# Latent attention's scores as one product over 128 rows a head

## The chip, the cores and the metric

The kernel runs on one core of a Trainium2 chip. Its time is device microseconds (us) from launch to end, the median of several runs; a profiled execution gives the rows below. Engines are named as in the profile: PE is TensorE's matmul stream and PEld its weight loads, DVE is VectorE, ACT is ScalarE, POOL is GpSimd, SP is SyncE, whose queue issues nearly all loads.

## The reference, cut to what matters

The model has two parts. The first is two layers on 256 tokens of width 1024. Each layer projects x by `w_in` (kept in HBM as streamed weights) and mixes three groups: a gated recurrence of 8 heads (HGRN2), latent attention of 8 heads (MLA), and cross-attention of 4 heads into a memory. Then comes an output product and a layer norm. The second part is one block of dilated attention and pooling, followed by a retrieval layer that gathers expert rows (8 heads of 16 for each token). Only the latent attention of the two layers is changed:

```python
q = (_rmsnorm(cq, q_norm) @ w_uq).reshape(B, S, 8, 64 + 32)
q_nope, q_rope = q[..., :64], _rope(q[..., 64:], cos, sin)
c = _rmsnorm(ckv, kv_norm)
k_nope = (c @ w_uk).reshape(B, S, 8, 64)
v = (c @ w_uv).reshape(B, S, 8, 64)
k_rope = _rope(kr, cos, sin)                  # one rotary key for all heads
s = (einsum('bqhd,bkhd->bhqk', q_nope, k_nope)
     + einsum('bqhr,bkr->bhqk', q_rope, k_rope)) / sqrt(96)
# causal mask, softmax, product with v
```

`_rope` multiplies the two halves of the 32 rotary channels by cosine and sine: `[t1*cos - t2*sin, t1*sin + t2*cos]`.

## The kernel before, in words

All weights of `w_in`, `w_out` and the memory projections come from HBM in half units of 128x1024 fp32 (512 KB), by SP, into `raw` (three buffers). ACT rounds each to `wh` (line 158), DVE forms the rest `wl` (line 159), and PE makes three products per pair of tiles from them (lines 212 to 214, `mm3`). `feature` (line 224) gives feature-major results, `token` (line 240) token-major ones. This stream of weights sets the order of the program.

Everything else in a layer is side work: Python generators in a list, `self.side`, that hand out instructions in pieces and name a cost for each piece (`yield 0.6`). Each half unit calls `tick`, which adds a credit of 1.4 (`PACE_A`) and takes pieces from the head of the list until the credit is spent. `finish(task)` writes out at once all that is left up to a task. `behind` (`bh` in the code) orders a DVE instruction behind the latest `wl` split on that engine. The final order on each engine is made by a list scheduler that goes by program order and modelled readiness.

For a layer the list starts with `mla_qkv` and `mla_rest` (projections of the latent attention), then the first recurrence pair, then `mla_attend`, later `finish(o0)` writes out what is left of `mla_attend`, of the second recurrence pair and of its output.

`mla_rest` transposes the normed latent rows into `cT` (line 498) and makes, from weights `ws` loaded once per layer: queries without rotation `qn` and rotary queries `qr`, six banks' halves of 128 columns (line 511, evicted by ACT at 513 and 515); keys `kn` (line 521) and values `v` (line 526), evicted by ACT; then it swaps the rotary halves of `qr` with a permutation product (line 531) and rotates on DVE (lines 535 to 538); then it transposes the rotary key (line 542), repeats it over 128 rows straight and swapped (lines 546, 547) and rotates it into `kr` (lines 550 to 552). PSUM banks come from `pps`, which has two.

`mla_attend` goes through `attend` eight times a layer: for each of the two query tiles of 128 tokens (`tt`), four groups of two heads, with 128 keys for the first tile and 256 for the second. A group's scores are two products a head, into one bank: 64 rows of `qn` and `kn` (line 562), then 32 rows of `qr` and `kr` (line 564) on top. DVE adds the causal mask (line 569), reduces and so on; transposes (436) and the product with `v` (460) follow.

An fp32 product stands as two PE records in the trace. `lnr`, the norm's rows for the end of the layer, shares the buffer of `ws` and is loaded by SP once the last product with `ws` is done (line 640).

Of the kernel before, what the change touches and what calls it, by code (L numbers as in the profile page):

```python
# [8 lines left out]
F = mybir.dt.float32  # L9
# [3 lines left out]
AF = mybir.ActivationFunctionType  # L13
OP = mybir.AluOpType
# [4 lines left out]
S = 256  # L19
D = 1024  # L20
# [76 lines left out]
def pack(inp):  # L97

    g = {k: np.asarray(v) for k, v in inp.items()}
    o = {}  # L100
    o["ca"], o["cb"] = _shape_constants()
    o["x"] = g["x"].reshape(2, 128, D).transpose(1, 0, 2)
    o["memT"] = g["mem"][0].T.reshape(8, 128, S).transpose(1, 0, 2)
    o["pos"] = g["positions"].reshape(1, S)
    wu, wm, ws = [], [], []
    for l in range(NL):
        w = g["w_in"][l]
        m = w[:, OCQ:OMG].reshape(2, 4, 128, 416).transpose(0, 2, 1, 3).reshape(2, 128, 1664)
        wm.append(m)
        u = _fm(g["w_mem_k"][l], 0, 512) + _tm(g["w_mem_v"][l], 0, 512)  # L110
        pair = lambda j: _fm(w, OF + 256 * j, 256) + _fm(w, OQ + 256 * j, 256)
        u += pair(0) + _tm(w, OI, 512) + pair(1) + _tm(w, OG, 512) + pair(2) + _tm(w, OI + 512, 512) + pair(3)
        u += _fm(w, OMQ, 512) + _tm(w, OG + 512, 512) + _tm(w, OMEMG, 512) + _tm(w, OMG, 512)
        wo = g["w_out"][l].reshape(4, 4, 128, 2, 512)
        for kg in KORD:
            for cg in range(2):
                u.append(wo[kg, :, :, cg].transpose(1, 0, 2).reshape(128, 2048))
        wu.append(np.stack(u))
        uq = g["w_mla_uq"][l].reshape(2, 128, 8, 96)
        uq = np.concatenate([uq[..., :64].reshape(2, 128, 512), uq[..., 64:].reshape(2, 128, 256)], axis=-1)  # L120
        ws.append(np.concatenate([uq.transpose(1, 0, 2).reshape(128, 1536), g["w_mla_uk"][l], g["w_mla_uv"][l]], axis=1))
    o["wu"], o["wm"], o["ws"] = np.stack(wu), np.stack(wm), np.stack(ws)
    o["rows1"] = np.concatenate([g["hgrn_out_norm"], g["mla_q_norm"], g["mla_kv_norm"], g["ln_g"], g["ln_b"]], axis=1)
    o["lnc"] = np.stack([g["ln_g"], g["ln_b"]], axis=1).reshape(2, 2, 8, 128).transpose(3, 0, 1, 2)
    o["lbl"] = g["hgrn_lb_logits"].reshape(2, 8, 128).transpose(2, 0, 1)
    cols = [g["c_2"].reshape(8, 128).T, g["norm1_g_2"].reshape(8, 128).T, g["norm2_g_2"].reshape(8, 128).T,
            g["pool_scale_2"].reshape(4, 128).T, g["b_ada_2"].reshape(48, 128).T]
    o["cols2"] = np.concatenate(cols, axis=1)
    o["rows2"] = np.concatenate([g["b_ada_2"][0, 2048:3072], g["b_ada_2"][0, 5120:6144], g["final_g_2"]]).reshape(1, 3072)
    o["wada"] = g["w_ada_2"][0].reshape(8, 128, 6, 1024).transpose(2, 0, 1, 3)  # L130
    w2 = g["w_in_2"][0]
    u = _fm(w2, 0, 1024) + _tm(w2, 1024, 1024)
    wo = g["w_out_2"][0].reshape(2, 4, 128, 2, 512)
    for kg in (1, 0):
        for cg in range(2):
            u.append(wo[kg, :, :, cg].transpose(1, 0, 2).reshape(128, 2048))
    u += _fm(g["peer_wq_2"][0], 0, 2048)
    o["wu2"] = np.stack(u)
    o["ws2"] = np.concatenate([g["pool_w_2"][0].transpose(1, 0, 2).reshape(128, 512),
                               g["peer_subkeys_2"][0].transpose(2, 0, 1).reshape(128, 256)], axis=1)  # L140
    o["puv"] = np.concatenate([g["peer_u_2"][0], g["peer_v_2"][0]], axis=1)
    return {k: np.ascontiguousarray(v) for k, v in o.items()}


class Prog:
# [346 lines left out]
    def mla_rest(self, ws, cn, out):  # L492
        nc, bh = self.nc, self.behind
        cT = self.ml.tile([128, 3, S], F, name="cT")
        for k in range(3):
            ps = self.pps.tile([128, S], F, name="bank")
# [1 line left out]
                nc.tensor.transpose(ps[:, tt * 128:(tt + 1) * 128], cn[:, tt, k * 128:(k + 1) * 128], self.ident)  # L498
            nc.scalar.activation(cT[:, k, :], ps, AF.Copy)
            yield 0.3  # L500
        sc = 1.0 / math.sqrt(96)
        qn = self.ml.tile([128, 4, S], F, name="qn")
        qr = self.ml.tile([128, 2, S], F, name="qr")
        kn = self.ml.tile([128, 4, S], F, name="kn")
        v = self.ml.tile([128, 2, 512], F, name="v")
        for j in range(3):
            ps = self.pps.tile([128, 2, S], F, name="bank")
            for m in range(2):
                for k in range(2):
                    c = k * 768 + (2 * j + m) * 128  # L510
                    nc.tensor.matmul(ps[:, m, :], ws[:, c:c + 128], cT[:, k, :], start=k == 0, stop=k == 1)
            if j < 2:
                nc.scalar.activation(qn[:, 2 * j:2 * j + 2, :], ps, AF.Copy, scale=sc)
            else:
                nc.scalar.activation(qr, ps, AF.Copy, scale=sc)
            yield 0.6
        for j in range(2):
            ps = self.pps.tile([128, 2, S], F, name="bank")
            for m in range(2):
                c = 1536 + (2 * j + m) * 128  # L520
                nc.tensor.matmul(ps[:, m, :], ws[:, c:c + 128], cT[:, 2, :], start=True, stop=True)
            nc.scalar.activation(kn[:, 2 * j:2 * j + 2, :], ps, AF.Copy)
            yield 0.6
        for tt in range(2):
            ps = self.pps.tile([128, 512], F, name="bank")
            nc.tensor.matmul(ps, cT[:, 2, tt * 128:(tt + 1) * 128], ws[:, 2048:2560], start=True, stop=True)
            nc.scalar.activation(v[:, tt, :], ps, AF.Copy)
            yield 0.6

        ps = self.pps.tile([128, 2, S], F, name="bank")  # L530
        nc.tensor.matmul(ps, self.perm, qr, start=True, stop=True)
        tmp = self.h2.tile([128, 2, S], F, name="pt")
        sb = self.sin[:, None, :].to_broadcast([128, 2, S])
        cb = self.cos[:, None, :].to_broadcast([128, 2, S])
        bh(nc.vector.tensor_tensor(tmp, ps, sb, op=OP.mult))
        bh(nc.vector.tensor_tensor(qr, qr, cb, op=OP.mult))
        yield 1.2
        bh(nc.vector.tensor_tensor(qr, qr, tmp, op=OP.add))
        yield 0.6
        ps = self.pps.tile([32, S], F, name="bank")  # L540
        for tt in range(2):
            nc.tensor.transpose(ps[:, tt * 128:(tt + 1) * 128], cn[:, tt, 384:416], self.ident)
# [2 lines left out]
        ps = self.pps.tile([128, 2, S], F, name="bank")  # L545
        nc.tensor.matmul(ps[:, 0, :], self.rep[:32, :], kr0, start=True, stop=True)
        nc.tensor.matmul(ps[:, 1, :], self.reps[:32, :], kr0, start=True, stop=True)
        kr = self.ml.tile([128, S], F, name="kr")
        tk = self.h2.tile([128, S], F, name="pt")
        bh(nc.vector.tensor_tensor(kr, ps[:, 0, :], self.cos, op=OP.mult))  # L550
        bh(nc.vector.tensor_tensor(tk, ps[:, 1, :], self.sin, op=OP.mult))
        bh(nc.vector.tensor_tensor(kr, kr, tk, op=OP.add))
        out += [qn, qr, kn, kr, v]
        yield 1.0

    def mla_attend(self, qkv, y):
# [72 lines left out]
    def layer(self, l, x, xt, mem):  # L629
        nc, I = self.nc, self.I  # L630
        W = I["wu"][l]
        rows = self.h4.tile([128, 512], F, name="rowsa", bufs=1)
        nc.sync.dma_start(rows, I["rows1"][l:l + 1, 0:512].to_broadcast([128, 512]))
        ws = self.ml.tile([128, 2560], F, name="ws")
        nc.sync.dma_start(ws, I["ws"][l])
        pm = self.misc(l, xt)
        qkv = []
# [35 lines left out]
        v = values()  # L673
# [3 lines left out]
        g = self.silu_gate(tok())  # L677
# [4 lines left out]
        v = values()  # L682
# [49 lines left out]
        if l == NL - 1:  # L732
            self.drain()
            self.ahead = self.unit(I["wu2"][0][:, 0:1024])
            ss = [self.sm.tile([128, 3], F, name="nss") for _ in range(2)]
        for tt in range(2):
            residual(tt, 0)
# [62 lines left out]
    def setup(self, cp, c0):  # L800
# [39 lines left out]
        self.pin = nc.scalar.preload_act_table_set("natural_log_exp_and_others")  # L840
        self.tc.add_manual_dep(self.pin.ins, last.ins.name, NOSYNC, reason="the set is loaded behind the sines")
        nc.vector.tensor_scalar(self.sin, self.sin, cols[:, 1:2], None, op0=OP.mult)

        lg = cp.tile([128, 2, 8], F, name="lg")
        nc.sync.dma_start(lg, I["lbl"])
# [378 lines left out]
def body(tc, I, O, stop=None):  # L1224
    nc = tc.nc
    p = Prog(tc, I)
    with tc.tile_pool(name="c0", bufs=1) as c0, tc.tile_pool(name="wp", bufs=3) as wp, \
# [4 lines left out]
        with tc.tile_pool(name="mo", bufs=1) as mo:  # L1232
            xnp = tc.alloc_tile_pool(name="xnp", bufs=1)
            gp = tc.alloc_tile_pool(name="gp", bufs=1)
            p.xn = xnp.tile([128, 2, D], F, name="xn")
            with tc.tile_pool(name="cp", bufs=1) as cp, tc.tile_pool(name="xtp", bufs=4) as xtp, tc.tile_pool(name="h4", bufs=3) as h4, \
                    tc.tile_pool(name="h2", bufs=2) as h2, tc.tile_pool(name="ml", bufs=1) as ml:
                p.xtp, p.h4, p.h2, p.ml = xtp, h4, h2, ml
# [47 lines left out]
```

## Time and profile before

| what | value |
|---|---|
| median of 3 runs | 1494.74 us (1493.81 to 1498.22) |
| the profiled execution | 1493.58 us, span of its instructions 1491.7 us |
| granted TensorE clock, mean | 0.941 |
| PE busy | 1298.4 us, 87% of the span |
| DVE busy | 998.4 us, 67% |
| ACT busy | 586.1 us, 39% |
| POOL busy | 241.3 us, 16% |

The two layers take about the first 640 us of the span, the second block and the retrieval the rest. Busy shares are averages over stages with different limits. A time in a row is counted from the span's start. In a row of the timeline the first number is the start, the second the length (overlapping where products are pipelined, so that costs are read from start to start), `x2` the number of records merged, and the bracket the idle time of that engine before the row with what ended it.

### The profile page before, as it was taken

Reading aid. Unit: us, or ns where it says so; the run is one execution under the profiler, and the core shown is the slowest. Engines: PE = TensorE matmul, PEld = TensorE weight load, DVE = VectorE, ACT = ScalarE, POOL = GpSimd, SP = SyncE. Lnnn points to the kernel's source line nnn. Section 1 sums busy time; section 2 is a strip of 40 time slices with the busy share of each in tenths; the row PEclk is TensorE's granted clock in tenths of the full one; section 3 lists DMA queues with packets and bytes.
Section 4 is the critical chain, followed back from the end, with each engine's and each line's share of the span. In section 5 each row is a group of like instructions: output and inputs, shape, how many; then the busy total and the mean of one; then the engine's idle time right before and its main releaser. Section 6 shows DMA issues by size and latency. Waiting matters only on the chain.

```text
span 1491.7 us, 17356 instructions
## 1 busy us (share of the span) xinstructions
PE 1298.4 (87%) x5834; PEld 883.0 (59%) x5834; DVE 998.4 (67%) x2037; ACT 586.1 (39%) x1282; POOL 241.3 (16%) x260
## 2 busy tenths in 40 slices
PE   8999999988999999989988976697887778777776
PEld 7888897877887988878777532233333333333332
DVE  6487688666678786667556899985554645555453
ACT  5556556535566676435444333321111311111112
POOL 0000000000000000000012322243333334333330
PEclk9999999999999999999999978889899899999988
DMA  8563255566562443476549798889999999999993
GB/s 287 164 213 116 85 171 174 180 217 214 177 197 73 142 141 121 155 234 205 162 140 412 277 394 320 333 339 422 420 421 422 422 420 422 421 421 422 422 421 153
DMA packets 74537, 404.79 MB, mean 271 GB/s; under 512 B 8912, under 2 KB 9296, under 8 KB 40784
## 3 DMA queue, kind: packets, MB, share of 16 engines
q0 software_dynamic: 36864, 268.45, 44.0%
q1 hardware_dynamic: 37584, 135.23, 28.0%
q8 instruction: 47, 0.77, 0.2%
q14 instruction: 42, 0.34, 0.1%
HBM read 402.60 MB, written 1.05 MB: 271 GB/s over the span
## 4 chain that ended last, share of the span: by engine, by line
PE 49%; DMA 30%; DVE 14%; ACT 4%; issue 4%; POOL 0%; POOLq 0%; DVEq 0%; ACTq 0%
DMA uv<-in_puv_dram,eid 26%; PE bank L213 10%; PE bank L212 10%; PE bank L214 10%; PE acc L1217 5%; DVE uv L1207 4%; DMA raw<-in_wu_dram 3%; PE bank L370 3%; ACT wh L158 2%; PE bank L460 2%; PE bank L220 1%; PE bank L564 1%; PE bank L562 1%; DVE wl L159 1%; PE bank L436 1%
## 5 line engine op out<-in xcount | busy, mean ns | idle before, releaser
L1217 PE MATMUL acc<-uv,d 128*128 128x512 f32 x1024 | 508.3, 655 | 141.4 <-ACT d L1215 141.4
L1217 PEld LDWEIGHTS acc<-uv,d 128*128 128x128 f32 x1024 | 209.5, 210 | 435.2 <-issue 248.3
L1207 DVE CUSTOM_DVE_ANT_0 uv<-hid,uv 128x1024 f32<-128x1024 f32 x256 | 312.7, 1225 | 216.7 <-DMA uv<-in_puv_dram,eid 209.9
L1173 POOL DMA_INDIRECT uv<-in_puv_dram,eid x256 | 241.1, 942 | 1212.0 <-ACT sc L1159 776.6
L159 DVE TENSOR_TENSOR wl<-raw,wh 128x1024 fp32r<-128x1024 f32 (+1 forms) x184 | 223.3, 1215 | 134.2 <-ACT wh L158 128.8
L158 ACT ACTIVATE wh<-raw 128x1024 fp32r<-128x1024 f32 (+1 forms) x184 | 192.7, 1050 | 201.5 <-DMA raw<-in_wu_dram 74.8
L1210 ACT ACTIVATE dot<-dot 128x4 f32<-128x4 f32 x64 | 13.1, 205 | 427.6 <-DVE dot L1207 427.6
L212 PE MATMUL bank<-wh,xh 128*128 128x512 f32 (+1 forms) x400 | 162.3, 406 | 1.8 <-ACT wh L158 1.1
L213 PE MATMUL bank<-wl,xh 128*128 128x512 f32 (+1 forms) x400 | 160.7, 402 | 2.2 <-DVE wl L159 2.2
L214 PE MATMUL bank<-wh,xl 128*128 128x512 f32 (+1 forms) x400 | 159.5, 400 | 0.0
L212 PE MATMUL bank<-xh,wh 128*128 128x256 f32 x384 | 112.6, 293 | 3.7 <-ACT wh L158 3.7
L214 PE MATMUL bank<-xh,wl 128*128 128x256 f32 x384 | 109.8, 286 | 6.0 <-DVE wl L159 6.0
L213 PE MATMUL bank<-xl,wh 128*128 128x256 f32 x384 | 109.8, 286 | 0.0
L1215 ACT ACTIVATE d<-ident,dot 128x128 f32<-128x128 f32 x256 | 82.3, 390 | 41.0 <-DVE dot L1211 36.9
L213 PEld LDWEIGHTS bank<-wl,xh 128*128 128x128 f32 x400 | 76.1, 190 | 19.2 <-DVE wl L159 4.2
L212 PEld LDWEIGHTS bank<-wh,xh 128*128 128x128 f32 x400 | 76.1, 190 | 17.2 <-ACT wh L158 1.5
L214 PEld LDWEIGHTS bank<-wh,xl 128*128 128x128 f32 x400 | 75.9, 190 | 15.7 <-issue 0.7
L214 PEld LDWEIGHTS bank<-xh,wl 128*128 128x128 f32 x384 | 72.9, 190 | 7.6 <-DVE wl L159 7.2
L212 PEld LDWEIGHTS bank<-xh,wh 128*128 128x128 f32 x384 | 72.9, 190 | 6.9 <-ACT wh L158 4.7
L213 PEld LDWEIGHTS bank<-xl,wh 128*128 128x128 f32 x384 | 73.0, 190 | 1.7 <-issue 1.2
L212 PE MATMUL bank<-nh,wh 128*128 128x256 f32 x192 | 58.3, 304 | 0.4 <-ACT nh L257 0.4
L213 PE MATMUL bank<-nl,wh 128*128 128x256 f32 x192 | 56.8, 296 | 1.8 <-DVE nl L258 1.4
(286 smaller groups left out, 1716.0 us busy)
## 6 DMA issues: line engine op xcount, KB each, us to landing
raw<-in_wu_dram SPq DMA_DIRECT2D x176, 512.0 KB, 4.3
raw<-in_wada_dram SPq DMA_DIRECT2D x48, 512.0 KB, 3.5
uv<-in_puv_dram,eid POOLq DMA_INDIRECT x256
raw<-in_wm_dram SPq DMA_DIRECT2D x8, 416.0 KB, 3.9
ws<-in_ws_dram SPq DMA_DIRECT2D x2, 1280.0 KB, 7.3
raw<-in_memT_dram SPq DMA_DIRECT2D x4, 512.0 KB, 4.5
lnr<-in_rows_dram SPq DMA_DIRECT2D x2, 1024.0 KB, 7.5
cb<-in_cb_dram SPq DMA_DIRECT2D x1, 1408.0 KB, 6.2
```

The costliest lines, as they stand in the source:

```text
L158: nc.scalar.activation(wh[:, :n], raw[:, :n], AF.Copy)
L159: self.last_split = nc.vector.tensor_tensor(wl[:, :n], raw[:, :n], wh[:, :n].bitcast(F), op=OP.subtract)
L212: mm(ps, a[0], b[0], start=start, stop=False)
L213: mm(ps, a[0], b[1], start=False, stop=False)
L214: self.last_mm = mm(ps, a[1], b[0], start=False, stop=stop)
L220: m = self.nc.tensor.matmul(ps, self.zero, self.zero[:, None, :].to_broadcast([128, 4, 128]), start=True, stop=True)
L370: nc.tensor.matmul(ps[:, h, k, :], st[:, c:c + 128], mv[:, c:c + 128], start=True, stop=True)
L460: nc.tensor.matmul(po[:, i, :], pt[:, i * kb + k, :], v[:, k, h * dv:(h + 1) * dv], start=k == 0, stop=k == kb - 1)
L1173: nc.gpsimd.indirect_dma_start(out=t, out_offset=None, in_=I["puv"], in_offset=bass.IndirectOffsetOnAxis(ap=eid[:, u, k:k + 1], axis=0))
L1207: nc.vector.tensor_tensor_reduce(out=uv[:, 0:D], in0=hid, in1=uv[:, 0:D], scale=1.0, scalar=0.0, op0=OP.mult, op1=OP.add, accum_out=dot[:, ...
L1215: nc.scalar.activation(d, self.ident, AF.Copy, scale=dot[:, u, k:k + 1])
L1217: nc.tensor.matmul(acc[:, cg * 512:(cg + 1) * 512], d, uv[:, D + cg * 512:D + (cg + 1) * 512], start=u % 8 == 0 and k == 0, stop=u % 8 == ...
```

## The change: what it does

The query weights are packed as 128 columns a head: 64 plain, 32 rotary, and the same 32 with swapped halves. One product stage gives `q` of 128 rows a head (four banks of two heads, where there were three); DVE evicts each bank with a multiplication by `turn`, a table of 128 rows made once in `setup` (the scale on 64 rows, scale times cosine on 32, scale times signed sine on 32). The permutation product and the three DVE operations on `qr` go. Keys get the same 128 rows: rows 64 to 127 of `kt` hold the rotated key twice, copied for all heads by ACT (two copies of 64x1024), rows 0 to 63 the plain key of each head, from products with 64 columns of weights (four banks of 64 rows, evicted by ACT). The score is then one product over 128 rows a head. The rotary key is made before the plain keys, and the values come last. The packed `ws` grows from 2560 to 3072 columns. `kt` lies in the buffer of `xn`, which is allocated only at the end of the second layer. The yields of `mla_rest` sum to 6.7 where they summed to 7.9.

```diff
@@ pack
-        uq = np.concatenate([uq[..., :64].reshape(2, 128, 512), uq[..., 64:].reshape(2, 128, 256)], axis=-1)
-        ws.append(np.concatenate([uq.transpose(1, 0, 2).reshape(128, 1536), g["w_mla_uk"][l], g["w_mla_uv"][l]], axis=1))
+        uq = np.concatenate([uq, uq[..., 80:], uq[..., 64:80]], axis=-1).reshape(2, 128, 1024)
+        ws.append(np.concatenate([uq.transpose(1, 0, 2).reshape(128, 2048), g["w_mla_uk"][l], g["w_mla_uv"][l]], axis=1))
@@ mla_rest
-        for j in range(3):
+        q = self.ml.tile([128, 8, S], F, name="q")
+        kt = self.xnp.tile([128, 8, S], F, name="kt", tag="xn")
+        for j in range(4):
             ps = self.pps.tile([128, 2, S], F, name="bank")
             for m in range(2):
                 for k in range(2):
-                    c = k * 768 + (2 * j + m) * 128
+                    c = k * 1024 + (2 * j + m) * 128
                     nc.tensor.matmul(ps[:, m, :], ws[:, c:c + 128], cT[:, k, :], start=k == 0, stop=k == 1)
-            if j < 2:
-                nc.scalar.activation(qn[:, 2 * j:2 * j + 2, :], ps, AF.Copy, scale=sc)
-            else:
-                nc.scalar.activation(qr, ps, AF.Copy, scale=sc)
+            bh(nc.vector.tensor_tensor(q[:, 2 * j:2 * j + 2, :], ps, self.turn[:, None, :].to_broadcast([128, 2, S]), op=OP.mult))
             yield 0.6
...
-        ps = self.pps.tile([128, 2, S], F, name="bank")
-        nc.tensor.matmul(ps, self.perm, qr, start=True, stop=True)
...
-        bh(nc.vector.tensor_tensor(tmp, ps, sb, op=OP.mult))
-        bh(nc.vector.tensor_tensor(qr, qr, cb, op=OP.mult))
-        yield 1.2
-        bh(nc.vector.tensor_tensor(qr, qr, tmp, op=OP.add))
-        yield 0.6
...
+        for j in range(2):
+            nc.scalar.activation(kt[64:, 4 * j:4 * j + 4, :], kr[64:, None, :].to_broadcast([64, 4, S]), AF.Copy)
+        for j in range(4):
+            ps = self.pps.tile([64, 2, S], F, name="bank")
+            for m in range(2):
+                c = 2048 + (2 * j + m) * 64
+                nc.tensor.matmul(ps[:, m, :], ws[:, c:c + 64], cT[:, 2, :], start=True, stop=True)
+            nc.scalar.activation(kt[:64, 2 * j:2 * j + 2, :], ps, AF.Copy)
+            yield 0.3
+        for tt in range(2):
...
+            nc.tensor.matmul(ps, cT[:, 2, tt * 128:(tt + 1) * 128], ws[:, 2560:3072], start=True, stop=True)
...
@@ mla_attend, score
-            a, c = h // 2, (h % 2) * 64
-            nc.tensor.matmul(ps, qn[c:c + 64, a, tt * 128:(tt + 1) * 128], kn[c:c + 64, a, :nk], start=True, stop=False)
-            a, c = h // 4, (h % 4) * 32
-            nc.tensor.matmul(ps, qr[c:c + 32, a, tt * 128:(tt + 1) * 128], kr[c:c + 32, :nk], start=False, stop=True)
+            nc.tensor.matmul(ps, q[:, h, tt * 128:(tt + 1) * 128], kt[:, h, :nk], start=True, stop=True)
@@ layer
-        ws = self.ml.tile([128, 2560], F, name="ws")
+        ws = self.ml.tile([128, 3072], F, name="ws")
@@ setup
+        sc = 1.0 / math.sqrt(96)
+        self.turn = cp.tile([128, S], F, name="turn")
+        nc.vector.memset(self.turn[:64, :], sc)
+        nc.vector.tensor_scalar(self.turn[64:96, :], self.cos[64:96, :], sc, None, op0=OP.mult)
+        nc.vector.tensor_scalar(self.turn[96:, :], self.sin[96:, :], sc, None, op0=OP.mult)
```

## Rows read from the trace of the kernel before

**Rows 1.** Windows: us, each engine's busy time (records), clock, DMA share, GB/s

```profile
52.00:66.00 14.00, 14.00 (x76) 11.53 (x75) 3.78 (x6) 7.15 (x12) 0.00 (x0) 1.00 0.33 98
...
427.00:537.00 110.00, 109.97 (x754) 93.83 (x753) 86.27 (x156) 68.22 (x162) 0.00 (x0) 1.00 0.40 129
```

**Rows 2.** Timeline of PE, layer 0, a score group of 128 keys

```profile
113.27 0.48 PE L562 MATMUL bank<-kn,qn 64*128 64x128 f32 x2
...
114.93 0.38 PE L212 MATMUL bank<-xh,wh 128*128 128x256 f32 x1
115.15 0.28 PE L213 MATMUL bank<-xl,wh 128*128 128x256 f32 x1
115.26 0.28 PE L214 MATMUL bank<-xh,wl 128*128 128x256 f32 x1
```

**Rows 3.** Timeline of PE, layer 1, a score group of 256 keys

```profile
456.78 0.70 PE L562 MATMUL bank<-kn,qn 64*128 64x256 f32 x2
457.40 0.69 PE L564 MATMUL bank<-kr,qr 32*128 32x256 f32 x2
...
459.28 1.05 PE L373 MATMUL bank<-qk 128*64 128x64 f32 x24
```

**Rows 4.** Group by form, both layers: busy us, mean ns | idle before

```profile
L513 ACT ACTIVATE qn<-bank 128x512 f32<-128x512 f32 x4 | 2.4, 597 | 5.6 <-PE bank L511 5.6
```

**Rows 5.** Chain that ended last, in order of time: start, us on the chain

```profile
53.66 4.75 PE bank L511 x22
58.41 0.86 PE bank L521 x4
...
101.38 0.89 PE bank L370 x8
```

**Rows 6.** Timeline of PE, layer 0, products with 32 columns of weights

```profile
73.20 0.40 PE L214 MATMUL bank<-wh,xl 128*128 128x512 f32 x1
73.44 0.38 PE L542 MATMUL bank<-ident,cn 128*32 128x128 f32 x2
...
73.89 0.40 PE L213 MATMUL bank<-wl,xh 128*128 128x512 f32 x1
```

**Rows 7.** Windows over the eight score groups of each layer, columns as above

```profile
113.20:174.00 60.80, 60.78 (x367) 49.34 (x365) 43.61 (x84) 34.94 (x87) 0.00 (x0) 0.92 0.29 94
430.20:486.80 56.60, 56.57 (x367) 45.40 (x365) 43.44 (x84) 34.94 (x87) 0.00 (x0) 1.00 0.31 100
```

**Rows 8.** Windows of PE alone, layer 0: us, PE busy, clock, DMA

```profile
140.00:142.00 2.00, 2.00 (x8) 1.00 0.01 4
...
144.00:146.00 2.00, 2.00 (x7) 0.50 0.56 203
```

**Rows 9.** Windows of 10 us, all engines, layer 1

```profile
410.00:420.00 10.00, 10.00 (x83) 9.11 (x82) 9.35 (x14) 6.40 (x13) 0.00 (x0) 1.00 0.72 217
```

**Rows 10.** Timeline of DVE, layer 1, the projections' stretch

```profile
375.70 1.22 DVE L159 TENSOR_TENSOR wl<-raw,wh 128x1024 fp32r<-128x1024 f32 x1 [4.76 <-PE bank L214]
...
382.51 0.69 DVE L535 TENSOR_TENSOR pt<-bank,sin 128x512 f32<-128x512 f32 x1 [2.48 <-PE bank L531]
```

**Rows 11.** DMA issues by tile: count, KB each, us to landing

```profile
ws<-in_ws_dram SPq DMA_DIRECT2D x2, 1280.0 KB, 7.3
```

**Rows 12.** Timeline of PE, start of layer 1

```profile
366.36 0.39 PE L212 MATMUL bank<-xh,wh 128*128 128x256 f32 x1 [2.75 <-ACT wh L158]
...
369.28 2.97 PE L511 MATMUL bank<-cT,ws 128*128 128x256 f32 x13
```

**Rows 13.** Timeline of SP, layer 0, and its issue of `ws` in layer 1

```profile
64.67 0.33 SPq L640 DMA_DIRECT2D lnr<-in_rows_dram  x1
71.65 0.99 SPq L166 DMA_DIRECT2D raw<-in_wu_dram  x2
...
359.22 0.33 SPq L635 DMA_DIRECT2D ws<-in_ws_dram  x1
```

**Rows 14.** Timeline of DVE, start of the kernel

```profile
23.14 0.17 DVE L851 TENSOR_TENSOR lgm<-lg 128x8 f32<-128x8 f32 x1 [0.86 <-ACT lg L849]
```

More of the change, by code (lines that the diff above doesn't have):

```diff
@@ L500, in mla_rest @@
             yield 0.3
[L501 to L504, printed above, removed]
+        q = self.ml.tile([128, 8, S], F, name="q")
+        kt = self.xnp.tile([128, 8, S], F, name="kt", tag="xn")
         v = self.ml.tile([128, 2, 512], F, name="v")
-        for j in range(3):
+        for j in range(4):
             ps = self.pps.tile([128, 2, S], F, name="bank")
@@ L509, in mla_rest @@
                 for k in range(2):
-                    c = k * 768 + (2 * j + m) * 128
+                    c = k * 1024 + (2 * j + m) * 128
                     nc.tensor.matmul(ps[:, m, :], ws[:, c:c + 128], cT[:, k, :], start=k == 0, stop=k == 1)
-            if j < 2:
-                nc.scalar.activation(qn[:, 2 * j:2 * j + 2, :], ps, AF.Copy, scale=sc)
-            else:
-                nc.scalar.activation(qr, ps, AF.Copy, scale=sc)
+            bh(nc.vector.tensor_tensor(q[:, 2 * j:2 * j + 2, :], ps, self.turn[:, None, :].to_broadcast([128, 2, S]), op=OP.mult))
             yield 0.6
-        for j in range(2):
-            ps = self.pps.tile([128, 2, S], F, name="bank")
[L519 to L522, printed above, removed]
-            yield 0.6
[L524 to L530, printed above, removed]
-        nc.tensor.matmul(ps, self.perm, qr, start=True, stop=True)
-        tmp = self.h2.tile([128, 2, S], F, name="pt")
-        sb = self.sin[:, None, :].to_broadcast([128, 2, S])
-        cb = self.cos[:, None, :].to_broadcast([128, 2, S])
-        bh(nc.vector.tensor_tensor(tmp, ps, sb, op=OP.mult))
-        bh(nc.vector.tensor_tensor(qr, qr, cb, op=OP.mult))
-        yield 1.2
-        bh(nc.vector.tensor_tensor(qr, qr, tmp, op=OP.add))
-        yield 0.6
         ps = self.pps.tile([32, S], F, name="bank")
@@ L547, in mla_rest @@
         nc.tensor.matmul(ps[:, 1, :], self.reps[:32, :], kr0, start=True, stop=True)
-        kr = self.ml.tile([128, S], F, name="kr")
         tk = self.h2.tile([128, S], F, name="pt")
+        bh(nc.vector.tensor_tensor(tk, ps[:, 1, :], self.sin, op=OP.mult))
+        kr = self.h2.tile([128, S], F, name="pt")
         bh(nc.vector.tensor_tensor(kr, ps[:, 0, :], self.cos, op=OP.mult))
-        bh(nc.vector.tensor_tensor(tk, ps[:, 1, :], self.sin, op=OP.mult))
         bh(nc.vector.tensor_tensor(kr, kr, tk, op=OP.add))
-        out += [qn, qr, kn, kr, v]
         yield 1.0
+        for j in range(2):
[8 more added lines that the diff above has]
+        for tt in range(2):
+            ps = self.pps.tile([128, 512], F, name="bank")
+            nc.tensor.matmul(ps, cT[:, 2, tt * 128:(tt + 1) * 128], ws[:, 2560:3072], start=True, stop=True)
+            nc.scalar.activation(v[:, tt, :], ps, AF.Copy)
+            yield 0.6
+        out += [q, kt, v]
     def mla_attend(self, qkv, y):
         nc = self.nc
-        qn, qr, kn, kr, v = qkv
+        q, kt, v = qkv
         def score(ps, h, tt, nk):
-            a, c = h // 2, (h % 2) * 64
-            nc.tensor.matmul(ps, qn[c:c + 64, a, tt * 128:(tt + 1) * 128], kn[c:c + 64, a, :nk], start=True, stop=False)
-            a, c = h // 4, (h % 4) * 32
-            nc.tensor.matmul(ps, qr[c:c + 32, a, tt * 128:(tt + 1) * 128], kr[c:c + 32, :nk], start=False, stop=True)
+            nc.tensor.matmul(ps, q[:, h, tt * 128:(tt + 1) * 128], kt[:, h, :nk], start=True, stop=True)
         def bias(s, ps, heads, tt):
@@ L734, in layer @@
             self.ahead = self.unit(I["wu2"][0][:, 0:1024])
+            self.xn = self.xnp.tile([128, 2, D], F, name="xn")
             ss = [self.sm.tile([128, 3], F, name="nss") for _ in range(2)]
@@ L1234, in body @@
             gp = tc.alloc_tile_pool(name="gp", bufs=1)
-            p.xn = xnp.tile([128, 2, D], F, name="xn")
+            p.xnp = xnp
             with tc.tile_pool(name="cp", bufs=1) as cp, tc.tile_pool(name="xtp", bufs=4) as xtp, tc.tile_pool(name="h4", bufs=3) as h4, \
```

## The prediction

> **What bounds the kernel now.** I read the page's slices first (PE full nearly all the way through the two layers), then windows over the stretches that the change touches, then PE's timeline around each changed product, then the chain that ended last for what one record costs, and DVE's and SP's timelines for what would be late next. The reader is to see three things. First, PE bounds the stretches of the change: it is busy for 14.00 of 14 us where the projections run and for 109.97 of 110 us from the attention on, at full clock, and the chain runs along PE there; DVE has 86.27 of the 110 and ACT 68.22 [rows 1]. Second, a product over 64 or 32 rows costs more than its columns. Third, DVE is not far behind PE in the attention itself [rows 7]. So a microsecond off PE counts until DVE is in the way.
>
> **Scores: removed work.** The prices go from start to start. A group of two heads with 128 keys has four products, two of 64 and two of 32 rows; it starts at 113.27, and the next work at 114.93: 1.66 us [rows 2]. With 256 keys it takes 459.28 - 456.78 = 2.50 us [rows 3], so 0.62 us a product, which is the distance between the two starts there. Products over all 128 rows cost less: 4.75 us for 22 records of 256 columns, 0.216 us each or 0.43 a product; 0.89 us for eight records of 128 columns, 0.111 each or 0.22 a product [rows 5]. So each switch between 64 and 32 rows costs 0.62 - 0.43 = 0.19 us above the streaming, and leaving the group costs once more: 0.22 us from 114.93 to 115.15 where the next like step takes 0.11 [rows 2]. After the change a group is two products over 128 rows: 0.44 us with 128 keys, 0.87 with 256. By the code there are four groups of each kind in a layer: 4 x (1.66 - 0.44) + 4 x (2.50 - 0.87) + 8 x 0.1 = 12.2 us off PE.
>
> **Projections: added work.** Queries: four banks for three, four products and so 8 records more, 8 x 0.216 = 1.73 us. Keys: eight products with 64 columns of weights for four with 128; the streamed columns per product stay 256, so 16 records for 8. One record cost 0.86 / 4 = 0.215 [rows 5], which adds 1.72 us if 64 columns are priced like 128. No row has 64 columns against 256 streamed. From below it can't be less than the streaming. From above, entering and leaving the 64-column shape might cost 0.19 us like the row switch; in at most four bursts that is 4 x 2 x 0.19 = 1.5 us a layer. The nearest row has 32 columns: from 73.20 to 73.89 there are two products of 512 columns (0.24 each, from 73.20 to 73.44, the first whole, the second up to the next start) and two records at 0.111, 0.70 in sum, and 0.69 passed [rows 6]. So no switch is seen there, and I take none. The Trainium skill (TensorEngine Tiling (Array Packing), Key Properties) says that changing the tiling mode drains TensorE. The score rows agree, with 0.19 us a change; the row with 32 columns does not, and by the rule the 64-column keys would take the gain down by 3.0 us over two layers. The permutation product goes: two records of 512 columns, priced by the same rows at 4 x 0.216 = 0.86 us. Net +2.6 us a layer.
>
> So PE has 12.2 - 2.6 = 9.6 us less a layer, 19.2 in both.
>
> **What DVE takes back.** The eight groups of layer 1 lie in 56.60 us, of which DVE is busy 43.44 [rows 7]. With 12.2 us less this would be 44.4 us, and DVE busy 98% of it. The highest share that I find over 10 us is 9.35 [rows 9]. At 93.5% the stretch needs 46.5 us, so 2.1 us of the saving are lost in each layer, 4.2 in both. Bounds: nothing (its work moves to the emptier stretch behind), and 6.7 us a layer, if it reaches only 85% (51.1 us).
>
> **The clock.** The same 367 PE records take 60.80 us in layer 0 and 56.60 in layer 1, where the clock is 1.00 against 0.92 [rows 7]: 4.2 us. In layer 0 PE had just run a group of 64- and 32-row products when the clock fell from 1.00 to 0.50, the 1.2 GHz level [rows 8]. Those groups go. But layer 1 ran the same groups without a fall, so they don't suffice for one; I take half, -2.1 us, and keep 0 and 4.2 as ends.
>
> **Edits taken at little or nothing.** DVE's queue: four multiplications of 0.69 us (the PSUM read of line 535 is the same shape [rows 10]) for three operations of that length, +0.7 us a layer, where DVE is busy 3.78 of 14 us [rows 1]; what it may hold up is a rival below. ACT: seven evictions of 0.597 us [rows 4] are 4.2; now two copies of 1024 elements (bounded by 2 x 0.597 each), four of 512 and the two for `v`, at most 6.0; its 7.15 of 14 us [rows 1] cover that, and uncovered it would be 1.8 us a layer. `ws` has a fifth more bytes: 7.3 us to land [rows 11] become 8.8 if all of it scales. In layer 0 PE is full behind it. In layer 1 PE sat idle 2.75 us for weights that share the DMA engines with `ws`, and the products with `ws` start at 369.28 [rows 12]; `ws`, issued at 359.22 [rows 13], landed at about 366.5 and would at about 368.0, so it is covered. For the weights I take 0.5 us, between 0 and 1.5. `lnr` now waits for values that are made last; SP's next load came 7.0 us behind it [rows 13], which covers it. If that cover is gone, `raw` loads stand behind it, and each microsecond beyond 7 is lost to PE. `turn` is three short DVE operations in `setup`, which the idle 0.86 us at 23.14 can hold [rows 14]; at worst that much is lost. Smaller yields let attention start up to one tick earlier; worth between 0 and 1.2 us a layer (the difference of the sums), taken as nothing.
>
> **Sum.** -19.2 + 4.2 - 2.1 + 0.5 = -16.6 us. The profiled execution took 1493.58 us (span 1491.7, 1.9 around it), so 1477.0; the median of the runs lies 1.2 above that execution, so 1478 us.
>
> **Rivals.**
>
> *DVE becomes the bound in the attention.* For it: the 43.44 us that don't shrink, and a chain from score to mask, maximum, exponentials and back to PE in each group. Against: 9.35 of 10 us were reached elsewhere. At 85% a layer saves 56.6 - 51.1 - 2.6 = 2.9 us: 5.8 + 2.1 - 0.5 = 7.4 us, so 1487 us. Should the share even stay near 80%, nothing is left (the stretch needs to lose 2.6 us, to 54.0, for the projections alone): about 1494.
>
> *The query banks wait on DVE (slower).* ACT evicted them on its own queue. Now each multiplication stands behind the latest weight split, and such a split waited 4.76 us for PE at 375.70 [rows 10], with nothing queued behind it that PE needed. With two banks in `pps`, the third and fourth bank of queries wait for these evictions, and the rotary key's and `ws` products behind them. Two such waits a layer are 4 x 4.76 = 19.0 us if PE finds nothing else: 1478 + 19 = 1497 us. It decides from 16.6 / 4 = 4.1 us a wait. Against it: those splits wait for stream products, which PE can take up in between, and DVE is mostly idle there.
>
> *The score products already overlap, so that one product saves nothing.* Then only the projections would show: 1494.7 + 5.2 = 1500 us. The starts, 0.62 us apart where full products are 0.43, speak against it. The Trainium skill (TensorEngine Tiling (Array Packing), Key Properties) has tiles in different row groups run in parallel, which speaks for it; the trace does not agree here, where each pair changes the mode.
>
> **How the numbers follow.** Chances: the forecast 0.62; DVE at some 85% 0.17; DVE taking all 0.06; query banks 0.11; overlap 0.02; something unnamed with small loss 0.02. The forecast's own range goes from 1469 (19.2 + 4.2 from the clock + 2.4 from the earlier start, 1493.6 - 25.8 + 1.2) to 1486 (DVE losses of 4 us a layer, no clock, 1.5 for `ws`, 0.9 in `setup`: 19.2 - 10.4 = 8.8 us); 3.0 for switches of the key products would make that 1489. To leave out no more than 2 in 10 it reaches to the DVE rival: 1469 to 1490. Faster by over 0.3% (4.5 us, about what this measurement can tell from no change): 0.62 + 0.17 + 0.01 = 0.80; within 0.3%: 0.07; slower: 0.13.
>
> **What would show it.** Right: score products of 0.22 and 0.43 us, start to start, with no extra at their edges; eight groups in about 47 us in either layer, DVE above 90% busy there; query products without PE idle before them; a clock of 1.00 over the groups of layer 0. Wrong: idle PE in front of lines 436, 460 or the stream while DVE is full; idle PE at the query banks with a DVE multiplication as its releaser; 64-column key records more than 0.216 us apart; `raw` loads late behind `lnr`. What would upset the sum most is the list scheduler: all side work of the layers is ordered anew, and a gap that the order before did not have costs as much as a term above.

## The result and the profile after

| | before | changed |
|---|---|---|
| median of the runs | 1494.28 us (4 runs, 1493.37 to 1498.22) | 1477.38 us (4 runs, 1474.12 to 1485.84) |
| profiled execution, its span | 1493.58, 1491.7 us | 1478.86, 1477.1 us |
| granted clock, mean | 0.941 | 0.944 |
| PE busy / DVE busy | 1298.4 / 998.4 us | 1277.1 / 998.9 us |

The ratio is 0.9891, with a 95% interval from 0.9845 to 0.9936: 1.1% faster. PE has 21.3 us less to do, DVE as much as before, and the span is 14.6 us shorter. The ratios leave out one run, of 4238.75 us at a mean clock of 0.283 in experiment 1.

PE's timeline at a group with 128 keys (layer 0) and at two with 256 keys, to be held against [rows 2] and [rows 3]:

```profile
117.03 0.61 PE L548 MATMUL bank<-kt,q 128*128 128x128 f32 x4
117.39 0.36 PE L212 MATMUL bank<-xh,wh 128*128 128x256 f32 x1
117.59 0.28 PE L213 MATMUL bank<-xl,wh 128*128 128x256 f32 x1
...
136.88 1.08 PE L548 MATMUL bank<-kt,q 128*128 128x256 f32 x4
137.62 0.58 PE L213 MATMUL bank<-wl,xh 128*128 128x512 f32 x1
...
144.03 1.08 PE L548 MATMUL bank<-kt,q 128*128 128x256 f32 x4
144.95 0.50 PE L370 MATMUL bank<-qk 128*128 128x128 f32 x3
```

A group is four records where it was eight. With 128 keys the first takes 0.36 us, and 0.56 to the second start of the work behind it (117.59), which was 1.88 us (113.27 to 115.15); the other three of the layer take 0.62 to 0.63 (121.47 to 122.10 in the second). With 256 keys the two shown take 0.74 and 0.92 us, which was 2.50.

Windows over the changed stretches: in each layer from the transposes of `cT` to the first score, then the groups, then the rest up to the first output of the gating. Columns are as in [rows 1]. First the projections' stretches of the kernel before, then all stretches of the changed one:

```profile
50.70:113.27 62.57, 62.57 (x399) 54.32 (x398) 43.65 (x63) 34.86 (x64) 0.00 (x0) 1.00 0.61 188
362.60:430.29 67.69, 64.94 (x421) 56.68 (x420) 46.07 (x66) 35.59 (x65) 0.00 (x0) 1.00 0.65 212
```

```profile
51.40:117.03 65.63, 65.32 (x414) 55.82 (x414) 43.95 (x63) 35.53 (x63) 0.00 (x0) 1.00 0.53 176
350.20:424.00 73.80, 69.93 (x435) 59.99 (x434) 46.21 (x66) 36.68 (x64) 0.00 (x0) 0.98 0.57 197
...
117.03:159.06 42.03, 41.32 (x319) 37.37 (x317) 37.87 (x79) 32.18 (x84) 0.00 (x0) 1.00 0.32 101
159.06:190.30 31.24, 29.64 (x244) 27.62 (x243) 25.18 (x48) 18.90 (x55) 0.00 (x0) 1.00 0.50 153
424.00:466.85 42.85, 41.51 (x320) 37.63 (x318) 38.08 (x79) 32.58 (x84) 0.00 (x0) 1.00 0.31 99
466.85:497.00 30.15, 29.54 (x232) 26.56 (x231) 25.45 (x48) 18.90 (x55) 0.00 (x0) 1.00 0.55 174
```

The clock is 1.00 through all groups, in layer 0 too, where it was 0.92 [rows 7]. PE is no longer quite full: in the four stretches from the first score on it stands idle for 0.71, 1.60, 1.34 and 0.61 us.

To have two executions of each kernel, experiments 1 and 4 below ran both again. In us, the first number of a pair being the execution shown so far:

| stretch | before | changed | difference |
|---|---|---|---|
| `cT` to first score, layer 0 | 62.57, 62.60 | 65.63, 65.80 | +3.1, +3.2 |
| `cT` to first score, layer 1 | 67.69, 69.00 | 73.80, 73.10 | +6.1, +4.1 |
| first score to gated output, layer 0 | 87.23, 85.70 | 73.27, 72.50 | -14.0, -13.2 |
| first score to gated output, layer 1 | 81.81, 84.70 | 73.00, 71.30 | -8.8, -13.4 |
| all the rest of the span | 1192.4, 1193.1 | 1191.4, 1189.6 | -1.0, -3.5 |
| span | 1491.7, 1495.1 | 1477.1, 1472.3 | -14.6, -22.8 |

The kernel before has these rows from the first score on (first execution; its groups alone are [rows 7]):

```profile
113.27:173.95 60.68, 60.66 (x366) 49.30 (x365) 43.54 (x84) 34.87 (x87) 0.00 (x0) 0.92 0.29 94
173.95:200.50 26.55, 26.43 (x232) 25.43 (x232) 20.37 (x42) 16.09 (x48) 0.00 (x0) 1.00 0.43 130
430.29:486.72 56.43, 56.40 (x365) 45.32 (x364) 43.35 (x84) 34.84 (x87) 0.00 (x0) 1.00 0.30 100
486.72:512.10 25.38, 25.38 (x211) 23.38 (x211) 20.66 (x42) 16.53 (x48) 0.00 (x0) 1.00 0.42 140
```

PE is idle for 0.17 us in them. So the time came from the attention, some of it went back into the projections, and the rest of the program moved by 1.0 and 3.5 us, where two executions of one kernel differ there by 0.7 and 1.8.

### The profile page after: what moved, and what is told of

The parts are those of the page before. It is cut to its first block, busy times and chain, and to the rows that moved or that the text cites. A ratio compares the mean times of both kernels' runs of the same rounds, so it can differ in the third digit from the quotient of the medians.

```text
span 1477.1 us, 17287 instructions
## 1 busy us (share of the span) xinstructions
PE 1277.1 (86%) x5798; PEld 874.0 (59%) x5798; DVE 998.9 (68%) x2042; ACT 588.3 (40%) x1284; POOL 243.9 (17%) x260
## 4 chain that ended last, share of the span: by engine, by line
PE 38%; DMA 35%; DVE 16%; issue 6%; ACT 4%; POOL 1%; POOLq 0%; DVEq 0%; ACTq 0%; SPq 0%
DMA uv<-in_puv_dram,eid 28%; PE bank L212 8%; PE bank L213 8%; PE bank L214 8%; DMA raw<-in_wu_dram 5%; DVE uv L1198 4%; ACT wh L158 2%; PE bank L370 2%; DVE wl L159 2%; PE bank L460 2%; PE bank L220 1%; POOL uv L1164 1%; PE acc L1208 1%; PE bank L509 1%; DVE si L1063 1%
## 5 line engine op out<-in xcount | busy, mean ns | idle before, releaser
L214 PE MATMUL bank<-xh,wl 128*128 128x256 f32 x384 | 113.1, 294 | 7.4 <-DVE wl L159 7.3
L889 DVE SCALAR_TENSOR_TENSOR macc<-raw,sc,macc 128x1024 f32<-128x1024 f32 x42 | 53.6, 1277 | 8.0 <-DMA raw<-in_wada_dram 7.9
## 6 DMA issues: line engine op xcount, KB each, us to landing
uv<-in_puv_dram,eid POOLq DMA_INDIRECT x256, 16.9
```

The source lines that it names most:

```text
L214: self.last_mm = mm(ps, a[1], b[0], start=False, stop=stop)
L889: self.behind(nc.vector.scalar_tensor_tensor(acc, raw, self.sc[:, k:k + 1], acc, op0=OP.mult, op1=OP.add))
```

## The experiments

**1. The changed kernel again** (no edit).

> The changed kernel as it is, once more, to separate what recurs from what one execution happens to show. The theory (short row groups cost 0.19 us a switch; DVE takes back part of it; the clock in the second layer's projections fell only because PE sat idle before it): the groups of each layer again in 42 to 43 us at a clock of 1.00, 73 us with what lies behind them, and again 3 us of idle PE at the start of the second layer. If the fall of the clock there recurs (0.66 over 5 us), it belongs to the change; if not, that 1.7 us was chance. Time 0.985 to 0.993 of the kernel before.

Measured: 1476.28 us median of 6 runs (five from 1474.09 to 1479.14, one of 4238.75), ratio 0.9875, interval 0.9844 to 0.9905. Windows over the same stretches as above:

```profile
116.70:159.00 42.30, 41.62 (x320) 37.64 (x319) 38.14 (x79) 32.45 (x84) 0.00 (x0) 1.00 0.32 102
159.00:189.20 30.20, 29.31 (x244) 27.38 (x243) 24.93 (x48) 18.70 (x54) 0.00 (x0) 1.00 0.49 157
421.40:463.70 42.30, 41.62 (x319) 37.72 (x318) 38.20 (x79) 32.56 (x84) 0.00 (x0) 1.00 0.31 103
463.70:492.70 29.00, 28.39 (x224) 25.44 (x223) 25.19 (x48) 18.63 (x54) 0.00 (x0) 1.00 0.52 177
...
349.00:354.00 5.00, 2.12 (x12) 1.92 (x12) 2.78 (x4) 1.65 (x4) 0.00 (x0) 0.81 0.98 401
354.00:359.00 5.00, 5.00 (x33) 4.82 (x32) 1.29 (x1) 1.44 (x2) 0.00 (x0) 0.85 0.76 263
```

The gain repeats, and so does the clock of 1.00 in the groups. PE's idle time from the first score to the gated output is 0.68 + 0.89 + 0.68 + 0.61 = 2.9 us, against 4.3 in the first execution. At the start of layer 1 PE waits for weights and the clock falls, here too.

**2. Keys of two heads from one product with 128 columns.** For odd heads the rows of `q` and `kt` are swapped (rotary first), so that one product gives the plain keys of an even head in rows 0 to 63 and of an odd one in rows 64 to 127. The 64-column shape is gone; the scores stay as they are. The edit also gives the table `turn` a second half for the odd heads, and lets the tile `mq` share the buffer of `cT`.

```diff
+        uq[:, :, 1::2] = np.concatenate([uq[:, :, 1::2, 64:], uq[:, :, 1::2, :64]], axis=-1)
...
-        for j in range(4):
-            ps = self.pps.tile([64, 2, S], F, name="bank")
+        for j in range(2):
+            ps = self.pps.tile([128, 2, S], F, name="bank")
             for m in range(2):
-                c = 2048 + (2 * j + m) * 64
-                nc.tensor.matmul(ps[:, m, :], ws[:, c:c + 64], cT[:, 2, :], start=True, stop=True)
-            nc.scalar.activation(kt[:64, 2 * j:2 * j + 2, :], ps, AF.Copy)
+                c = 2048 + (2 * j + m) * 128
+                nc.tensor.matmul(ps[:, m, :], ws[:, c:c + 128], cT[:, 2, :], start=True, stop=True)
+            for o in range(2):
+                nc.scalar.activation(kt[64 * o:64 * o + 64, 4 * j + o:4 * j + 4:2, :], ps[64 * o:64 * o + 64], AF.Copy)
```

> The changed kernel, but heads of odd number keep the rotary rows in rows 0 to 63 and the plain rows in 64 to 127, so that one product with 128 columns of weights gives the keys of two heads (four products a layer for eight), and no product has 64 columns. Theory (a product costs its streamed columns, plus some 0.15 to 0.2 us where the shape changes): eight records of 0.216 and three bursts of about 0.35 us less, 2.7 us off PE a layer, 5 us in both: 0.986 of the kernel before. Rival (64-column products run at half price, and the shape change costs nothing): no difference to the changed kernel, 0.989. Rival (the projections are not what bounds the second layer): 2.7 us in all.

Measured: 1474.64 us median (1471.65 to 1478.36), ratio 0.9859, interval 0.9831 to 0.9888. From `cT` to the first mask it takes 64.3 us in layer 0 and 71.7 in layer 1, where experiment 1 took 66.5 and 73.8: 2.2 and 2.1 less. PE's timeline at the key products, first of the changed kernel, then of this one:

```profile
65.32 1.08 PE L533 MATMUL bank<-cT,ws 128*64 128x256 f32 x4
66.33 0.38 PE L212 MATMUL bank<-xh,wh 128*128 128x256 f32 x1
66.55 0.28 PE L213 MATMUL bank<-xl,wh 128*128 128x256 f32 x1
66.67 0.28 PE L214 MATMUL bank<-xh,wl 128*128 128x256 f32 x1
66.87 1.94 PE L533 MATMUL bank<-cT,ws 128*64 128x256 f32 x8
68.75 0.38 PE L212 MATMUL bank<-xh,wh 128*128 128x256 f32 x1
```

```profile
66.39 1.13 PE L536 MATMUL bank<-cT,ws 128*128 128x256 f32 x4
67.17 0.47 PE L214 MATMUL bank<-xh,wh 128*128 128x256 f32 x1
```

With 64 columns four records take 1.01 us (65.32 to 66.33) and eight 1.88 (66.87 to 68.75), where 0.215 each gives 0.86 and 1.72: about 0.15 us on entering the shape. On leaving, the next step takes 0.22 us (66.33 to 66.55) where the like step after it takes 0.12: 0.10 more. The Trainium skill (TensorEngine Tiling (Array Packing), Key Properties) says that a change of tiling mode drains TensorE; these rows agree. Three such bursts a layer cost 3 x 0.25 = 0.75 us. Streaming that halves (1.72 us) and those switches would make 2.5 us a layer, of which 2.2 and 2.1 are seen. In the first burst, where 32-row products stand ahead of the keys in both kernels, the 64 columns cost only 0.15: 1.23 us to the second start behind it (65.32 to 66.55) against 1.08 (66.39 to 67.47). Of the versions that do all the work this one has the lowest median, but its interval overlaps that of experiment 1. Its profiled execution is only 0.9 us ahead when both layers are nearly done (601.9 us against 602.8), since other stretches took longer, and loses 3.9 us behind that, where the edit changes nothing.

**3. The modulation's additions on POOL instead of DVE.** Over both layers they are DVE's largest work behind the weight splits: 32 additions of 1.28 us in the changed kernel, 40.9 us.

```diff
-                self.behind(nc.vector.scalar_tensor_tensor(acc, raw, self.sc[:, k:k + 1], acc, op0=OP.mult, op1=OP.add))
+                nc.gpsimd.tensor_scalar(raw, raw, self.sc[:, k:k + 1], None, op0=OP.mult)
+                nc.gpsimd.tensor_tensor(acc, acc, raw, op=OP.add)
```

> The changed kernel, but the running sum for the second block's modulation (one 128x1024 operation of 1.28 us on DVE at every third tick) is made on POOL, as a multiplication and an addition. Theory (DVE, busy 90% of the groups' stretch, takes back 2.4 us in layer 0 and 3.4 us in layer 1): it returns, the 73 us of groups and what lies behind them become 70 to 71 in each layer, and the time 5 us less, 0.986. Rival (the order on PE takes it back, not DVE): no difference, 0.989. Rival (POOL is slow and raw buffers come free late, so that weights are late): slower than the changed kernel by 5 us or more.

Measured: 1566.34 us median (1560.73 to 1576.99), ratio 1.0478, interval 1.0439 to 1.0517. Lines on POOL in layer 0, then what engines waited for in both layers:

```profile
L889 POOL TENSOR_SCALAR raw<-raw,sc 128x1024 f32<-128x1024 f32 x14 | 45.4, 3239 | 223.3 <-DMA raw<-in_wada_dram 118.0 <-DMA raw<-in_wu_dram 85.1 <-DVE qk L359 12.1
L890 POOL TENSOR_TENSOR macc<-macc,raw 128x1024 f32<-128x1024 f32 x14 | 37.6, 2685 | 1.2
```

```profile
DVE wl L159 <- ACT wh L158: 133.1, 66, 8.4
ACT wh L158 <- DMA raw<-in_wu_dram: 103.7, 46, 7.6
```

One addition holds its `raw` buffer for 3.24 + 2.69 = 5.9 us instead of 1.28. There are three such buffers for the whole stream, so the loads of the weights start late: ACT waits for them 103.7 us in all, where it waited 49.8 in the changed kernel, and DVE and PE wait behind it. So the last of the expectations came, with 90 us against experiment 1 instead of some 5. It says nothing on DVE as a bound; experiment 7 asks that again without moving work.

**4. The kernel before again** (no edit, one execution).

> The kernel before as it is, once more. Theory (the short row groups of layer 0 bring the clock down): the clock is again below 1.00 between 140 and 170 us, and the eight groups of layer 0 take about 4 us longer than those of layer 1 (60.8 and 56.6). Rival (the fall was chance): both layers take 56 to 57 us, or it falls in another layer.

Measured: 1497.01 us, span 1495.1. Windows over its groups and the stretches behind them, and over single places:

```profile
113.00:170.80 57.80, 57.78 (x365) 46.63 (x364) 43.31 (x84) 34.83 (x87) 0.00 (x0) 0.97 0.32 99
170.80:198.70 27.90, 27.79 (x231) 26.70 (x231) 20.33 (x41) 16.20 (x48) 0.00 (x0) 0.94 0.41 125
426.60:484.50 57.90, 57.87 (x365) 46.69 (x364) 43.29 (x84) 34.79 (x87) 0.00 (x0) 0.97 0.30 98
484.50:511.30 26.80, 26.80 (x212) 24.87 (x212) 20.68 (x42) 16.57 (x48) 0.00 (x0) 0.94 0.40 132
...
162.00:164.00 2.00, 2.00 (x9) 1.85 (x9) 1.60 (x3) 0.96 (x4) 0.00 (x0) 0.50 0.25 59
...
360.00:365.00 5.00, 3.68 (x20) 3.68 (x21) 1.56 (x2) 1.99 (x4) 0.00 (x0) 0.72 0.97 366
```

In this execution the clock falls in both layers while PE is full, once in the groups and once behind, and the groups of layer 0 take no longer than those of layer 1: it isn't tied to layer 0, as the theory had it. At 0.50, the 1.2 GHz level, stream products start 0.21 us apart instead of 0.12 (356 to 359 us in the changed kernel). What the falls cost is read against the stretches of the first execution that ran at 1.00 with the same products: 57.80 + 27.90 + 57.90 + 26.80 us here, 56.43 + 26.55 + 56.43 + 25.38 there, 5.6 us. In the first execution it was 60.68 - 56.43 = 4.25 us, all in layer 0. The fall at the start of layer 1 is in the last row (360 to 365), so it belongs to the kernel before as well.

**5. The second head's two products in reverse order, in the kernel before.** 64, 32, 32, 64 rows instead of 64, 32, 64, 32: the same products, with one change between 64 and 32 rows less in a group; it ends on 64 rows instead of 32.

```diff
...
-            nc.tensor.matmul(ps, qn[c:c + 64, a, tt * 128:(tt + 1) * 128], kn[c:c + 64, a, :nk], start=True, stop=False)
...
-            nc.tensor.matmul(ps, qr[c:c + 32, a, tt * 128:(tt + 1) * 128], kr[c:c + 32, :nk], start=False, stop=True)
...
+            parts = [(qn[c:c + 64, a, t], kn[c:c + 64, a, :nk]), (qr[o:o + 32, e, t], kr[o:o + 32, :nk])]
+            for i, (w, x) in enumerate(parts[::-1] if h >= 4 else parts):
+                nc.tensor.matmul(ps, w, x, start=i == 0, stop=i == 1)
```

> The kernel before, but the second head of each group makes its 32-row product first and its 64-row product last, so that two products of 32 rows stand side by side and a group has one change of shape less; the work is the same. Theory (0.19 us for each change of shape): a group of 256 keys takes 2.31 us from start to start instead of 2.50, one of 128 keys 1.47 instead of 1.66; 16 groups give 3.0 us, 0.998. Rival (a product of few rows costs 0.62 us by itself, whatever stands before it): 2.50 and 1.66 us as before, no difference.

Measured: 1490.18 us median of 10 runs against 1493.48 of 13, ratio 0.9985, interval 0.9955 to 1.0015: 16 groups at 0.19 us are 3.0 us, and the medians are 3.3 apart, which is within what the times can't tell from nothing. The timeline of PE in a 128-key group can:

```profile
113.30 0.48 PE L565 MATMUL bank<-kn,qn 64*128 64x128 f32 x2
113.72 0.71 PE L565 MATMUL bank<-kr,qr 32*128 32x128 f32 x4
114.35 0.49 PE L565 MATMUL bank<-kn,qn 64*128 64x128 f32 x2
114.77 0.39 PE L212 MATMUL bank<-xh,wh 128*128 128x256 f32 x1
```

The group takes 1.47 us (113.30 to 114.77) where it took 1.66 [rows 2], and 2.31 us with 256 keys (449.57 to 451.88) where it took 2.50 [rows 3]. The two middle products together take 0.63 us (113.72 to 114.35), their streaming 0.44 and one change of 0.19. So the change of rows is what costs, 0.19 us with 128 keys and with 256. The two middle products don't overlap, but they use the same 32 rows of the array; two products on different rows never stand side by side without a change of shape here.

**6. Queries evicted by ACT, as before; their rotation is left out.**

```diff
-            bh(nc.vector.tensor_tensor(q[:, 2 * j:2 * j + 2, :], ps, self.turn[:, None, :].to_broadcast([128, 2, S]), op=OP.mult))
+            nc.scalar.activation(q[:, 2 * j:2 * j + 2, :], ps, AF.Copy, scale=1.0 / math.sqrt(96))
```

> The changed kernel, but ACT evicts the query banks with the scale alone, and DVE has no multiplication there; this leaves the rotation of the queries out. Theory (PE never waits for those evictions; the projections cost what their records cost): query records 0.216 us apart as now, no difference in time beyond 1 us, 0.989. Rival (evictions behind the weight splits hold the banks up): 4 us or more faster, 0.986 or less.

Measured: 1480.68 us median (1477.78 to 1481.33), ratio 0.9903, interval 0.9870 to 0.9937: no gain. In the changed kernel the timeline shows the queries on PE, and then DVE's evictions:

```profile
54.17 6.64 PE L509 MATMUL bank<-cT,ws 128*128 128x256 f32 x30
60.46 0.47 PE L214 MATMUL bank<-xh,wl 128*128 128x256 f32 x1
```

```profile
55.67 0.69 DVE L510 TENSOR_TENSOR q<-bank,turn 128x512 f32<-128x512 f32 x1 [2.13 <-PE bank L509]
57.40 0.69 DVE L510 TENSOR_TENSOR q<-bank,turn 128x512 f32<-128x512 f32 x1 [1.03 <-PE bank L509]
```

PE goes through all four banks without a gap, and it is DVE that waits for PE, about 1 us at a bank. Removing DVE from this place has nothing to give back.

**7. Seven of eight modulation additions left out** (their loads stay).

```diff
-                self.behind(nc.vector.scalar_tensor_tensor(acc, raw, self.sc[:, k:k + 1], acc, op0=OP.mult, op1=OP.add))
+                pass
```

> The changed kernel, but seven of eight additions of the running sum for the second block's modulation are left out (the loads stay): 5.1 us less of DVE work in each layer's stretch of the groups and behind them, on no other engine more. Theory (DVE takes back 2.4 and 3.4 us there): these 73 us become about 70 in each layer, some 5 us or a little more in all, 0.985. Rival (DVE is busy there but not in the way; the order of the side work on PE takes it back): 73 us as now, no difference, 0.989.

Measured: 1458.98 us median (1454.92 to 1462.19), ratio 0.9769, interval 0.9736 to 0.9802. Windows over the groups and the stretches behind them, and over `cT` to the first score of layer 1:

```profile
116.60:156.60 40.00, 40.00 (x300) 35.99 (x300) 34.40 (x73) 31.75 (x82) 0.00 (x0) 1.00 0.37 121
156.60:187.60 31.00, 30.63 (x260) 28.88 (x260) 24.95 (x51) 18.68 (x55) 0.00 (x0) 1.00 0.38 121
413.20:453.20 40.00, 39.99 (x301) 36.01 (x300) 34.38 (x73) 31.79 (x82) 0.00 (x0) 1.00 0.37 127
453.20:483.30 30.10, 29.73 (x242) 26.98 (x242) 25.43 (x51) 18.77 (x55) 0.00 (x0) 1.00 0.44 139
...
344.40:413.20 68.80, 67.98 (x435) 58.43 (x434) 40.62 (x61) 36.39 (x64) 0.00 (x0) 1.00 0.60 203
```

Groups and stretch behind take 71.0 and 70.1 us, about what the theory expected. The whole, 0.977 instead of 0.985, is far below it: of the 19.1 us to the execution of experiment 1, 2.7 lie in these stretches, 4.3 at the start of layer 1, 2.3 in the rest of layer 0, and 9.7 behind 602.8 us, where additions of the same kind are left out too. In the groups PE's idle time is gone, and with the stretch behind there is 0.8 us of it left in both layers together, against 4.3 and 2.9 in the changed kernel. So 2.1 to 3.5 us of the gain are lost to this load on DVE. The groups themselves are 2.3 us a layer shorter, but some of that is other products (some 20 records less inside) that PE now does behind them. The start of layer 1 shrinks too: from 73.80 and 73.10 us to 68.80, idle from 3.9 and 3.4 to 0.8 us, with no fall of the clock. What PE waits for there is the weight stream, as it does in the kernel before (2.75 us [rows 12]). What removes the wait is seen only as another order on PE: in experiment 7 the queries (from 347.40) stand ahead of the products of the load that PE waited for (354.12), in the changed kernel behind them (354.39, queries from 359.54). Whether `raw` buffers that come free earlier have a part in it isn't shown.

## Why the prediction was right, step by step

It gave 1478 us (1469 to 1490), and 1477.38 was measured. The two traces are 14.7 us apart where the sum said 16.6, the medians 16.9 and, in experiment 1, 19.7. The terms:

*Scores, -24.4 us in both layers: right in mechanism, 1 to 2 us too large.* To the second start behind it, one group in four with 128 keys takes 0.56 us, about the price set (0.44 + 0.11), and the others 0.62 to 0.63; with 256 keys the slower of the two shown takes 0.92 where 0.87 was set. At 0.06 and 0.05 us a group that is some 0.9 us in both layers. From the windows: PE's busy time from the first score to the gated output fell from 168.87 to 142.01 us, and in the second pair from 170.24 to 140.95; less the clock's 4.25 and 5.6 us (experiment 4) that is 22.6 and 23.7. Where the rest went, up to 1 us, perhaps to other products at the ends of the stretches, isn't settled. That the 0.19 us is the change of rows is shown by experiment 5.

*Projections, +5.2: short by the keys.* The sum was right for the queries (0.216 us a record). I took nothing for the 64-column shape because a 32-column row showed no switch; the keys' own rows show 0.75 us a layer, which experiment 2 gives back in the main. With it the forecast is 3.35 us a layer; in layer 0 3.1 and 3.2 were measured, 0.3 of each being idle PE. The bound from above, 1.5 us a layer, held.

*What DVE takes back, +4.2: the size was about right, the path to it not.* PE's idle time grew by 4.1 us in the first pair of executions and 2.7 in the second. In the first execution it stands in front of lines 436, 460 and the stream, which the prediction had named as a sign of being wrong, and of line 370, in waits of 0.3 to 0.8 us. But the groups did not stop at 46.5 us with DVE 93.5% busy: they take 42 to 43 us with DVE at 37.87 / 42.03 = 90%. Stream products that stood among the groups moved behind them instead, and the stretch behind grew from 26.55 to 31.24 us in layer 0 and from 25.38 to 30.15 in layer 1. A share of DVE inside a stretch with movable ends is no good measure; idle PE over the stretch and what follows it is.

*The clock, -2.1: too small.* I took half because layer 1 ran without a fall. One execution had misled: in experiment 4 layer 1 falls as well. The two executions lost 4.25 and 5.6 us, and both of the changed kernel nothing there. The end of the range, 4.2, was too near. That the short-row groups cause the fall is not shown: experiment 5 kept them all and had 1.00 from 112 to 174 us and from 426 to 506. And experiment 6, whose scores are the changed kernel's, fell to 0.50 behind its groups (180 to 182 us, PE busy for 2.00 of 2). So this part of the gain may be the chance of the executions that were profiled.

*`ws`, `lnr` and weights, +0.5: about right.* `ws` lands in 10.0 us, not 8.8, but was issued at 347.02 and its first product starts at 359.54: covered. PE's longest wait for the weights is 2.96 us after 2.75, and all of its idle time from `cT` to the first score of layer 1 is 3.87 after 2.75, in the second pair 3.38 after 2.70. The rows at the start of layer 1, changed kernel:

```profile
354.39 0.39 PE L212 MATMUL bank<-xh,wh 128*128 128x256 f32 x1 [2.96 <-ACT wh L158]
```

```profile
355.00:360.00 5.00, 5.00 (x31) 4.95 (x30) 1.88 (x2) 0.81 (x2) 0.00 (x0) 0.66 0.78 308
```

Behind the wait the clock is 0.66 for 5 us; 16 stream products in a row take 3.40 us there (355.67 to 359.07), 1.5 more than at 0.12 each. That is about half of what layer 1 lost beyond layer 0 in the first pair (6.1 against 3.1), and the idle time half of the rest; in the second pair, where both kernels fall there, 4.1 stand against 3.2. So a forecast held against two executions with the same falls would have been off by less.

*The sum.* The scores (0.7 to 1.8 less than taken), the keys (+1.5) and this fall (+1.5) on one side, the clock in the groups (2.1 to 3.5 more than taken) on the other: the total came out within a microsecond of the median partly by luck, because these misses have opposite signs.

*Rivals.* Score products that overlap: refuted by the result, as PE's busy time fell with the products. The second and third groups of the kernel before put a head's 64 and 32 rows on different rows of the array, and take 1.65 and 1.66 us (121.30 to 122.95, 127.22 to 128.88), as long as the first, where they are the same rows (1.66). Query banks that wait on DVE: refuted by PE's gapless rows and experiment 6. DVE as the bound in these stretches: only 2.1 to 3.5 us of it (experiment 7), where its time of 1487 needs 6.7 a layer, 13.4 in both.

## What to carry to other kernels

Price a small product by the distance to the next start and compare it with a product over the full array: what stands above the streaming is the change of shape, and it is paid in both directions, for rows and, here, for 64 columns. Where an engine close behind the bound might take back a gain, look for idle time of the bounding engine over the stretch and its successor together, since a scheduler moves work over the border. Profile the kernel before more than once if a term hangs on the clock: three executions with the short rows lost 4.25, 5.6 and nothing in these stretches.

## What was not expected of the hardware

The clock fell to 0.50 (162 to 164 us in experiment 4) while PE was busy for 2.00 of 2 us; being busy did not prevent it. Both executions of the changed kernel ran at 1.00 through their groups, but so did experiment 5 with all short-row products. The 64-column shape pays 0.15 us on entry and 0.10 on leaving, though in [rows 6] the 32-column one pays nothing that can be seen. On POOL a multiplication of 128x1024 fp32 took 3.24 us and an addition 2.69 (means of 14 in layer 0), for what DVE does in one operation of 1.28 us.
